# A decoder trunk in fp32r: every tile that products read moves to a multiple of 512 bytes in its partition

## The chip, the cores and the metric

The kernel runs on one core of a Trainium2 chip. The metric is the device time of one execution in microseconds (us). Before the change three runs gave 3106.07, 3107.32 and 3114.94 us, a median of 3107.32. One more execution was taken with the profiler; its own time is 3115.24 us, and its span from the first to the last instruction 3113.5 us.

A core has five engines that run side by side and wait for each other through semaphores: TensorE (PE in the profile, with the weight loads apart as PEld), VectorE (DVE), ScalarE (ACT), GpSimd (POOL) and SyncE (SP), which here only issues DMAs. SBUF is the on-chip memory of 128 partitions; a tile [P, N] takes N elements in each of the 128 partitions, at the same byte offset in all of them. PSUM is the memory that TensorE writes.

## What is computed

Two decoder layers over 1024 tokens of width 1024, all in fp32. Each layer computes `x <- LN(alpha*x + mixer(x))` and then `x <- LN(alpha*x + MLP(x))`, the MLP with 4096 hidden units and a squared ReLU. The mixer of layer 0 is a gated DeltaNet with 8 heads of 128 (short convolution on q, k and v, then a chunked delta rule); that of layer 1 is S5, a complex diagonal state-space layer. Beside each mixer runs a 4-head cross-attention into 256 memory tokens, and both share an input and an output projection. For the change, S5 matters: 64 groups of 16 channels each drive 64 complex states,

```
h_t = Abar * h_(t-1) + Bbar u_t        (per group, elementwise in the state)
y_t = Re(C h_t) + D u_t
```

## The kernel before, in words

**Products.** A weight or activation that goes into a wide product is split into a high part, rounded to the type fp32r, and a low part, the rest, also fp32r. `mm3` (lines 111 to 116) then makes one fp32 product of three fp32r products, high x high, high x low and low x high, added up in PSUM. The wide products have 128 x 128 weights and 512 moving columns; those of the memory keys (mk) and of the attention scores (sc) have 256. `proj_fm` (line 122) multiplies 128 output features at a time with the transposed activations xT: 8 slices of 128 input features, two halves of 512 tokens, so 48 products for one block of weights. `acc_tm` (line 138) multiplies token tiles with the second MLP weights or the output projection and adds to y. DeltaNet's chunk products and S5's are in plain fp32 and have 128 columns; the trace shows two PE instructions for each of those.

**Order.** `run` (line 1165) goes through: the first input projections and gates; memory keys and values and attention of layer 0 among the first DeltaNet keys; the eight DeltaNet heads (`gdn_b`, with `conv_silu` at line 384 for q, k and v); the output projection and layer norm; the first MLP (14 blocks of two hidden tiles and one of four); memory keys and values of layer 1; S5 with the attention of layer 1; the GLU; the second output projection; the second MLP. PE works through its products in that order. Beside the first MLP, `s5_side` (line 1254) puts the preparation of S5 behind each MLP block: tables, coefficients (`s5_coeffs`) and the matrices of S5 (`s5_mats`, line 1039), which POOL's DMA queue writes to DRAM.

**S5.** A sequence of 1024 tokens is cut into 128 chunks of 8, so that time runs over 128 columns, and a tile has 8 groups. `s5_u` (line 1067) projects the input of 8 groups and writes it to DRAM as ud; `s5_core` (line 1077) of the same 8 groups loads it as u. In u each group has a row of 129 columns: column 0 is set to zero by DVE (line 1083), columns 1 to 128 are the 128 chunks (line 1084). The products p1 and p2 (lines 1107 to 1110) read columns 0 to 127, the chunk before; DVE's scan (line 1118) runs the state over the columns; three products add up to py: M0, which works within a chunk, reads columns 1 to 128 of u (line 1125), and H1 and H2 read the rotated states r1 and r2 (lines 1126, 1127). H1 comes from `combine` (line 1002) in `s5_mats`: three DVE operations over [128, 4 groups, 9 lags, 16], 576 elements, in the tag h5. Lags 0 to 7 go into the product pz (line 1052), followed for each group by a product with dd, which DVE makes after H1 (line 1136); lags 1 to 8 are what `s5_core` later loads (line 1099). POOL's queue writes all nine to DRAM in one DMA (line 1048).

**Memory.** Two pools lie in SBUF, constants (`cp`) and then work tiles (`sp`). The work pool has a fixed number of buffers per tag (line 50), each as long as the tag's longest tile; every tile of a tag lies in one of its buffers. The allocator goes in steps of 32 bytes. The program of the kernel before has these byte offsets, given as the rest after division by 512:

| tag or tile | what lies there | length of a buffer | offset within 512 |
|---|---|---|---|
| ident (constant) | identity for transposes, at 16512 | 512 | 128 |
| scr | masks, gate values, S5 powers, at 17984 | 5280 | 64 |
| h1, raw, w1 | second MLP weights (half), loads, first weights | 2048, 4096, 4096 | 224 |
| xT (6 buffers) | activations high and low, keys, y, S5's s5t | 16448 | 224, 288, 352, 416, 480, 32 |
| gb (2) | convolution input, norms, S5 coefficients | 4128 | 96, 128 |
| S (6) | DeltaNet's states and the like, dd | 512 | 160 |
| h5 (5) | S5 matrices, some MLP weights | 2304 | 160, 416 in turn |
| h2, h3, h4 | second MLP weights (half), hidden parts, attention | 2048 | 416 |

Slices that products take within a tile begin at multiples of 512 bytes from the tile's start, with these exceptions: u's rows in s5t (129 columns, 516 bytes apart, read from column 0 or column 1), H1's groups (576 bytes apart), and weights of 32 columns or fewer.

Of the kernel before, what the change touches and what calls it, by code (L numbers as in the profile page):

```python
# [10 lines left out]
F32 = mybir.dt.float32  # L11
# [5 lines left out]
P = 128  # L17
T = 1024
# [10 lines left out]
class Trunk:  # L29
    def __init__(self, ctx, tc, a):  # L30
        self.tc = tc
        self.nc = nc = tc.nc
        self.a = a
        self.uid = 0
        self.turn = 0
        self.proj = 0
        self.cp = ctx.enter_context(tc.tile_pool(name="cp", bufs=1))
        self.sp = ctx.enter_context(tc.tile_pool(name="sp", bufs=1))
        self.ps = ctx.enter_context(tc.tile_pool(name="ps", bufs=1, space=bass.MemoryType.PSUM))
        self.dp = ctx.enter_context(tc.tile_pool(name="dp", bufs=1, space=bass.MemoryType.DRAM))  # L40
        self.ident = self.const("ident", [P, P])
        make_identity(nc, self.ident)
        self.eps_ln = self.const("eps_ln", [P, 1])
        nc.gpsimd.memset(self.eps_ln, 1e-5)
        self.mhalf = self.const("mhalf", [P, 4])
        nc.gpsimd.memset(self.mhalf, -0.5)
        self.half = self.const("half", [P, 4])
        nc.gpsimd.memset(self.half, 0.5)
# [172 lines left out]

    def gdn_consts(self):
        nc = self.nc
        scr = self.tile("scr", [P, 3 * P + 8 + 13 * 64 + 96], F32, "scr")
        masks = [scr[:, n * P:(n + 1) * P] for n in range(3)]
        self.small = [scr[:, 3 * P + 8 + n * 64:3 * P + 8 + (n + 1) * 64] for n in range(13)]
        early = self.tile("h1", [P, 3 * P], F32, "early")
        U = early[:, 0:P]
        nc.gpsimd.memset(U, 1.0)
        nc.gpsimd.affine_select(U, U, [[1, P]], ALU.is_ge, 0.0, base=0, channel_multiplier=-1)  # L230
        self.U = U
        ones = early[:, P:2 * P]
        nc.gpsimd.memset(ones, 1.0)
        self.ones = ones
        mn = masks[0]
        nc.gpsimd.memset(mn, 0.0)
        nc.gpsimd.affine_select(mn, mn, [[1, P]], ALU.is_ge, -1e30, base=0, channel_multiplier=-1)
        self.maskneg = mn

        m64 = masks[1]  # L240
        nc.gpsimd.memset(m64, 0.0)
        nc.gpsimd.memset(m64[0:32, 32:64], 1.0)
        nc.gpsimd.memset(m64[64:96, 96:128], 1.0)
        m128 = masks[2]
        nc.gpsimd.memset(m128, 0.0)
        nc.gpsimd.memset(m128[0:64, 64:128], 1.0)
        self.m64, self.m128 = m64, m128
        bd = scr[:, 3 * P:3 * P + 4]
        nc.gpsimd.memset(bd, 0.0)
        for b in range(4):  # L250
            nc.gpsimd.memset(bd[32 * b:32 * b + 32, b:b + 1], 1.0)
        self.bdm = bd
        self.early = [early[:, 2 * P + 64 * n:2 * P + 64 * (n + 1)].rearrange("p (t h) -> p t h", t=8) for n in range(2)]
        cw = scr[:, 3 * P + 8 + 13 * 64:].rearrange("p (m j) -> p m j", j=4)
        nc.sync.dma_start(cw, self.a["cw"])
        self.cw = cw
        ng = self.const("ng", [P, 1])
        nc.sync.dma_start(ng, self.a["ng"])
        nc.gpsimd.tensor_scalar(ng, ng, 0.5, None, op0=ALU.mult)
        self.ng = ng  # L260
        self.kdd = self.dp.tile([8, 2, P, 4, P], F32, tag="kdd", name="kdd")
        self.ded = self.dp.tile([8, 2, P, 4, P], F32, tag="ded", name="ded")
        self.ntf = self.dp.tile([8, 2, 2, P, 4, P], F32, tag="ntf", name="ntf")
        self.ntd = self.dp.tile([8, 8, 4, 32, 32], F32, tag="ntd", name="ntd")
        self.t32 = self.dp.tile([2, 8, 8, 4, 32, 32], F32, tag="t32", name="t32")
# [118 lines left out]
    def conv_silu(self, m, xT, outs, tag, w=None):  # L384

        nc = self.nc
        cv = self.tile("gb", [P, 3 + T], F32, "cv")
        nc.vector.memset(cv[:, 0:3], 0.0)

        def evac(h, ps):  # L390
            b = h * HALF
            nc.scalar.copy(cv[:, 3 + b:3 + b + HALF], ps)
            o = outs[h]
            w = self.cw[:, m, :]
            nc.scalar.activation(o, ps, AF.Copy, scale=w[:, 3:4])
            for j in range(3):
                nc.vector.scalar_tensor_tensor(o, cv[:, b + j:b + j + HALF], w[:, j:j + 1], o, op0=ALU.mult, op1=ALU.add)
            th = self.tile(tag, [P, HALF], F32, "th")
            nc.scalar.activation(th, o, AF.Tanh, scale=0.5)
            nc.vector.scalar_tensor_tensor(o, th, 1.0, o, op0=ALU.add, op1=ALU.mult)  # L400

        self.proj_fm(w or self.a["w_in"][m], xT, evac, "wi")
# [596 lines left out]
        nc.gpsimd.memset(z, 0.0)  # L999
        nc.gpsimd.dma_start(self.zd[:, :, :, 0:112].rearrange("m i g x -> (m i) g x"), z)  # L1000

    def combine(self, eng, x, y, pr, pi, op, b, nm):

        n = pr.shape[1]
        o, w = (self.tile("h5", [P, 4, n, 16], F32, z) for z in (nm, "cw"))
        gs = slice(4 * b, 4 * b + 4)
        xb, yb = (z[:, gs, :].unsqueeze(2).to_broadcast([P, 4, n, 16]) for z in (x, y))
        pr, pi = (z.rearrange("p d g -> p g d").unsqueeze(3).to_broadcast([P, 4, n, 16]) for z in (pr, pi))
        eng.tensor_tensor(o, xb, pr, op=ALU.mult)
        eng.tensor_tensor(w, yb, pi, op=ALU.mult)  # L1010
        eng.tensor_tensor(o, o, w, op=op)
        return o
# [26 lines left out]
    def s5_mats(self, m, b, co):  # L1039

        nc = self.nc
        V = nc.vector
        A_, S_ = ALU.add, ALU.subtract
        flat = lambda x: x.rearrange("p a b -> p (a b)")
        re, im = (z[:, :, 8 * m:8 * m + 8] for z in self.pw)
        gs = gl = slice(4 * b, 4 * b + 4)
        h1 = self.combine(V, co[:, 2], co[:, 3], re[:, :, gl], im[:, :, gl], A_, b, "H1")
        nc.gpsimd.dma_start(self.h1d[m, :, gs], h1)
        dd = self.dd(8 * m + 4 * b)
        pz = self.psum("pa", "pz", (P, 4, 8, 16))  # L1050
        for g in range(4):
            nc.tensor.matmul(flat(pz[:16, g]), co[:, 0, 4 * b + g, :], flat(h1[:, g, 0:8, :]), start=True, stop=False)
            nc.tensor.matmul(pz[:16, g, 0, :], self.ident[:16, :16], dd[:, g, :], start=False, stop=True)
        z = self.tile("h5", [P, 4, 8, 16], F32, "z")[:16]
        nc.scalar.copy(z, pz[:16])
# [21 lines left out]
    def s5_core(self, m):  # L1077

        nc = self.nc
        V, G = nc.vector, nc.gpsimd  # L1080
        M, A_ = ALU.mult, ALU.add
        u = self.s5t[:, 2 * T + 8 * 129 * (m % 2):2 * T + 8 * 129 * (m % 2 + 1)].rearrange("p (g n) -> p g n", g=8)
        V.memset(u[:, :, 0:1], 0.0)
        nc.sync.dma_start(u[:, :, 1:129], self.ud[m].rearrange("s (i g) n -> (s i) g n", i=16))
        M0 = self.s5t[:, T:2 * T].rearrange("p (g x) -> p g x", g=8)
        z = self.zd[m]
        nc.sync.dma_start(M0, bass.AP(z.tensor, z.offset, [[16, 8], [8 * 240, 16], [240, 8], [1, P]]))
        for b in range(2):
            gs = slice(4 * b, 4 * b + 4)
# [7 lines left out]
            G1 = load("h1", "G1", self.g1d[m, :, gs])  # L1097
            tab = [load("h2", "tab", self.tabd[x, :, g0:g0 + 4, :]) for x in range(2)]
            H1 = load("h2", "H1", self.h1d[m, :, gs, 1:9, :].rearrange("p g d o -> p g (d o)"))
            H2 = load("h2", "H2", self.h2d[m, :, gs])  # L1100

            p1 = self.psum("pa", "p1", (P, 4, P))
            p2 = self.psum("pa", "p2", (P, 4, P))
            G2 = self.tile("h1", [P, 4, P], F32, "G2")
            nc.scalar.copy(G2[:, :, 0:64], G1[:, :, 64:128])
            nc.scalar.copy(G2[:, :, 64:128], G1[:, :, 0:64])
            for g in range(4):
                nc.tensor.matmul(p1[:, g, :], G1[:, g], u[:, 4 * b + g, 0:128], start=True, stop=True)
            for g in range(4):
                nc.tensor.matmul(p2[:, g, :], G2[:, g], u[:, 4 * b + g, 0:128], start=True, stop=True)  # L1110
            t1 = self.tile("h3", [P, 4, P], F32, "t1")
            t2 = self.tile("h3", [P, 4, P], F32, "t2")
            V.tensor_tensor(t1, p1, tab[0], op=M)
# [2 lines left out]
            w = self.tile("h3", [P, 4, P], F32, "wsc")  # L1116
            for g in range(4):
                V.tensor_tensor_scan(w[:, g, :], self.r8[:, g0 + g:g0 + g + 1].to_broadcast([P, P]), t1[:, g, :], 0.0, M, A_)
            r1 = self.tile("h1", [P, 4, P], F32, "r1")
            r2 = self.tile("h1", [P, 4, P], F32, "r2")  # L1120
# [1 line left out]
            G.tensor_tensor(r2, w, tab[1], op=M)  # L1122
            py = self.psum("pi", "py", (P, 4, P))
            for g in range(4):
                nc.tensor.matmul(py[:, g, :], M0[:, 4 * b + g, :], u[:, 4 * b + g, 1:129], start=True, stop=False)
                nc.tensor.matmul(py[:, g, :], H1[:, g], r1[:, g, :], start=False, stop=False)
                nc.tensor.matmul(py[:, g, :], H2[:, g], r2[:, g, :], start=False, stop=True)  # L1127
            zg = self.tile("h3", [P, 4, P], F32, "zg")
            nc.scalar.activation(zg, py, AF.Gelu_apprx_tanh)
            nc.sync.dma_start(self.yd[m].rearrange("s (o g) n -> (s o) g n", o=16)[:, gs, :], zg)  # L1130
# [34 lines left out]
    def run(self):  # L1165
# [39 lines left out]
        self.cat = d("cat1", [1536, T])  # L1205
        xT = self.mlp_block(0, y, xT, self.s5_side, lambda tau: nc.sync.dma_start(self.x2[tau], y[tau]), True)
        kv = self.mem_kv(1)
        self.s5t = self.tile("xT", [P, 2 * T + 2 * 8 * 129], F32, "s5t")
        self.s5_u(0, xT)
        for m in range(8):  # L1210
            if m < 7:
# [129 lines left out]
```

## Time and profile before

| | before |
|---|---|
| median of three runs | 3107.32 us |
| the profiled execution, its own time | 3115.24 us |
| its span | 3113.5 us |
| instructions | 36492 |
| mean granted TensorE clock | 0.967 of full |
| DMA | 288.11 MB in 204145 packets |

How to read the views that follow. The page's first lines give each engine's busy time and its share of the span, then, as a digit for each of 40 slices, tenths of full speed for the clock. The view of stretches has one row per stretch of time: its length, then busy microseconds and, in brackets, the instruction count of PE, PEld, DVE, ACT and POOL, the granted clock, the DMA share and GB/s. The view of groups has one row per line, engine and operands: shape, count, then busy time, mean ns of one instruction, idle time of its engine just before, and who ended it. The view of order gives start, duration, engine, line and operands, with `x8` where neighbours of one kind are merged. Matmuls are pipelined: one is under way while the next starts, so a duration is not the time that one more costs; the difference of two starts is.

### The profile page before, as it was taken

To read this page: it belongs to the slowest core of one execution; us is meant where nothing else is said; L and a number is where in the kernel's file an instruction comes from. 1 tells how busy PE (TensorE), PEld (TensorE's weight loads), DVE (VectorE), ACT (ScalarE), POOL (GpSimd) and SP (SyncE) were. 2 spreads that over 40 slices of the span, in tenths; PEclk is the share of its full clock that TensorE was granted. 3 is DMA by queue.
4 is the path that set the end of the run, shared out by engine and by line. 5 is a ranking of instruction groups with operands and counts; after the bars stand their busy time and mean duration, and the time that the engine had idled before them with its cause. 6 is when DMAs were issued, how large, how long until landed. Compare 5 with 4: busy or idle time off the path is not lost. (4 is left out here: it accounts for less than half of the span.)

```text
span 3113.5 us, 36492 instructions
## 1 busy us (share of the span) xinstructions
PE 2892.1 (93%) x13629; PEld 2311.9 (74%) x13629; DVE 1762.9 (57%) x3452; ACT 964.6 (31%) x2070; POOL 488.4 (16%) x729
## 2 busy tenths in 40 slices
PE   8789898898998999999999989987999999999998
PEld 6568676676777888777777767765777888888876
DVE  7635766765578677666663733443467344334436
ACT  5334444443422322232222222332222222222221
POOL 3620633625001021110100100011000000000001
PEclk9889999999999999999999999998999999999999
DMA  5322433333522133222221365554321111111111
GB/s 193 101 58 82 115 105 101 99 105 77 179 82 76 42 108 92 83 97 73 87 85 62 103 183 168 167 144 142 108 95 61 48 48 43 53 48 48 41 48 54
DMA packets 204145, 288.11 MB, mean 93 GB/s; under 512 B 85776, under 2 KB 126944, under 8 KB 203968
## 3 DMA queue, kind: packets, MB, share of 16 engines
q1 hardware_dynamic: 188864, 245.46, 25.7%
q0 software_dynamic: 12800, 36.13, 3.9%
q10 hardware_dynamic: 2304, 4.20, 0.4%
q8 instruction: 107, 1.75, 0.2%
q14 instruction: 70, 0.57, 0.1%
HBM read 213.93 MB, written 71.79 MB: 92 GB/s over the span
## 5 line engine op out<-in xcount | busy, mean ns | idle before, releaser
L213 DVE TENSOR_TENSOR y<-tm,y 128x512 f32<-128x512 f32 x448 | 308.5, 690 | 223.0 <-PE tm L116 217.4
L114 PE MATMUL w<-xTh,w1h 128*128 128x512 f32 x1024 | 409.7, 400 | 14.9 <-ACT w1h L93 14.9
L116 PE MATMUL w<-xTh,w1l 128*128 128x512 f32 x1024 | 407.4, 398 | 4.5 <-DVE w1l L94 4.4
L114 PE MATMUL tm<-w2h,hh 128*128 128x512 f32 x1024 | 406.7, 398 | 0.0
L115 PE MATMUL w<-xTl,w1h 128*128 128x512 f32 x1024 | 406.6, 397 | 0.0
L116 PE MATMUL tm<-w2h,hl 128*128 128x512 f32 x1024 | 403.6, 395 | 0.0
L115 PE MATMUL tm<-w2l,hh 128*128 128x512 f32 x1024 | 402.1, 393 | 0.0
L106 ACT CAST w2h<-w2r 128x512 fp32r<-128x512 f32 x128 | 76.3, 619 | 588.7 <-PE tm L116 506.0
L114 PEld LDWEIGHTS w<-xTh,w1h 128*128 128x128 f32 x1024 | 194.1, 190 | 60.0 <-ACT w1h L93 16.2
L116 PEld LDWEIGHTS w<-xTh,w1l 128*128 128x128 f32 x1024 | 194.5, 190 | 52.0 <-DVE w1l L94 6.3
L115 PEld LDWEIGHTS w<-xTl,w1h 128*128 128x128 f32 x1024 | 194.2, 190 | 45.1
L116 PEld LDWEIGHTS tm<-w2h,hl 128*128 128x128 f32 x1024 | 192.1, 188 | 47.4 <-DVE hl L202 0.3
L114 PEld LDWEIGHTS tm<-w2h,hh 128*128 128x128 f32 x1024 | 192.2, 188 | 45.8 <-ACT hh L201 1.3
L115 PEld LDWEIGHTS tm<-w2l,hh 128*128 128x128 f32 x1024 | 192.7, 188 | 44.7
L167 POOL TENSOR_SCALAR mv<-mv 128x1 f32<-128x1 f32 x32 | 25.0, 780 | 1246.8 <-DVE mv L166 1246.8
L202 DVE TENSOR_TENSOR hl<-w,hh 128x512 fp32r<-128x512 f32 x128 | 87.2, 687 | 188.6 <-ACT hh L201 188.6
L94 DVE TENSOR_TENSOR w1l<-w1r,w1h 128x1024 fp32r<-128x1024 f32 x64 | 78.3, 1224 | 184.7 <-ACT w1h L93 184.7
L114 PE MATMUL wi<-xTh,wih 128*128 128x512 f32 x384 | 159.3, 415 | 3.5 <-ACT zc L640 3.5
L115 PE MATMUL wi<-xTl,wih 128*128 128x512 f32 x384 | 158.7, 413 | 0.0
L116 PE MATMUL wi<-xTh,wil 128*128 128x512 f32 x384 | 156.4, 407 | 0.0
L197 ACT ACTIVATE w<-w 128x512 f32<-128x512 f32 x128 | 74.5, 582 | 188.0 <-PE w L116 188.0
L93 ACT CAST w1h<-w1r 128x1024 fp32r<-128x1024 f32 x64 | 67.2, 1050 | 198.8 <-PE w L115 157.4
(414 smaller groups left out, 5791.3 us busy)
## 6 DMA issues: line engine op xcount, KB each, us to landing
w2r<-in_w_dram SPq DMA_DIRECT2D x64, 512.0 KB, 3.5
w1r<-in_w_dram SPq DMA_DIRECT2D x64, 512.0 KB, 3.5
wir<-in_w_in_dram SPq DMA_DIRECT2D x24, 512.0 KB, 3.7
wor<-in_w_o_dram SPq DMA_DIRECT2D x24, 512.0 KB, 3.5
cat<-cat SPq DMA_DIRECT2D x24, 512.0 KB, 3.4
gb<-gcd SPq DMA_DIRECT2D x32, 256.0 KB, 4.5
ntf<-nm POOLq DMA_DIRECT2D x32, 256.0 KB, 3.0
nm<-ntf SPq DMA_DIRECT2D x32, 256.0 KB, 3.4
```

The costliest lines, as they stand in the source:

```text
L93: nc.scalar.copy(hi, r)
L94: nc.vector.tensor_tensor(lo, r, f32(hi), op=ALU.subtract)
L106: nc.scalar.copy(hi, s)
L114: nc.tensor.matmul(ps, a[0], b[0], start=start, stop=False)
L115: nc.tensor.matmul(ps, a[0], b[1], start=False, stop=False)
L116: nc.tensor.matmul(ps, a[1], b[0], start=False, stop=stop)
L167: nc.gpsimd.tensor_scalar(mv[:, 2:3], mv[:, 1:2], 1e-5, None, op0=ALU.add)
L197: nc.scalar.activation(ps, ps, AF.Relu)
L202: nc.vector.tensor_tensor(lo, ps, f32(hi), op=ALU.subtract)
L213: nc.vector.tensor_tensor(o, ps, o, op=ALU.add)
```

## The change

The constants are padded, and the work pool begins at 18432: a tile of 448 bytes is added behind ident, and the constants then add up to 1920 bytes from 16512. Buffers whose length was no multiple of 512 become one: scr 5632 bytes, gb 4608, xT 16384, h5 2048. The lengths of the others stay. For xT, S5's u has rows of 128 columns without the zero column: p1 and p2 read all 128, so their states are those of one chunk later, and the shift by one chunk moves to H1 and H2, which multiply columns 0 to 126 of r1 and r2 and write columns 1 to 127 of py. For h5, H1 is made in two calls of `combine`: lags 0 to 7 in h5 as before, lag 8 in the tag S (three DVE operations over 64 elements), each with a DMA of its own on POOL's queue. The memset of u's zero column goes, and the load of u fills a contiguous piece of 4 KB in each partition.

```diff
         make_identity(nc, self.ident)
+        self.const("pad", [P, 112])
         self.eps_ln = self.const("eps_ln", [P, 1])
...
-        scr = self.tile("scr", [P, 3 * P + 8 + 13 * 64 + 96], F32, "scr")
+        scr = self.tile("scr", [P, 11 * P], F32, "scr")[:, :3 * P + 8 + 13 * 64 + 96]
...
-        cv = self.tile("gb", [P, 3 + T], F32, "cv")
+        cv = self.tile("gb", [P, T + P], F32, "cv")[:, :3 + T]
...
-    def combine(self, eng, x, y, pr, pi, op, b, nm):
+    def combine(self, eng, x, y, pr, pi, op, b, nm, tag="h5"):
         n = pr.shape[1]
-        o, w = (self.tile("h5", [P, 4, n, 16], F32, z) for z in (nm, "cw"))
+        o, w = (self.tile(tag, [P, 4, n, 16], F32, z) for z in (nm, "cw"))
...
-        h1 = self.combine(V, co[:, 2], co[:, 3], re[:, :, gl], im[:, :, gl], A_, b, "H1")
-        nc.gpsimd.dma_start(self.h1d[m, :, gs], h1)
+        h1 = self.combine(V, co[:, 2], co[:, 3], re[:, 0:8, gl], im[:, 0:8, gl], A_, b, "H1")
+        nc.gpsimd.dma_start(self.h1d[m, :, gs, 0:8], h1)
+        h8 = self.combine(V, co[:, 2], co[:, 3], re[:, 8:9, gl], im[:, 8:9, gl], A_, b, "H8", "S")
+        nc.gpsimd.dma_start(self.h1d[m, :, gs, 8:9], h8)
...
-            nc.tensor.matmul(flat(pz[:16, g]), co[:, 0, 4 * b + g, :], flat(h1[:, g, 0:8, :]), start=True, stop=False)
+            nc.tensor.matmul(flat(pz[:16, g]), co[:, 0, 4 * b + g, :], flat(h1[:, g]), start=True, stop=False)
...
-        u = self.s5t[:, 2 * T + 8 * 129 * (m % 2):2 * T + 8 * 129 * (m % 2 + 1)].rearrange("p (g n) -> p g n", g=8)
-        V.memset(u[:, :, 0:1], 0.0)
-        nc.sync.dma_start(u[:, :, 1:129], self.ud[m].rearrange("s (i g) n -> (s i) g n", i=16))
+        u = self.s5t[:, (2 + m % 2) * T:(3 + m % 2) * T].rearrange("p (g n) -> p g n", g=8)
+        nc.sync.dma_start(u, self.ud[m].rearrange("s (i g) n -> (s i) g n", i=16))
...
-                nc.tensor.matmul(p1[:, g, :], G1[:, g], u[:, 4 * b + g, 0:128], start=True, stop=True)
+                nc.tensor.matmul(p1[:, g, :], G1[:, g], u[:, 4 * b + g, :], start=True, stop=True)
...
-                nc.tensor.matmul(p2[:, g, :], G2[:, g], u[:, 4 * b + g, 0:128], start=True, stop=True)
+                nc.tensor.matmul(p2[:, g, :], G2[:, g], u[:, 4 * b + g, :], start=True, stop=True)
...
-                nc.tensor.matmul(py[:, g, :], M0[:, 4 * b + g, :], u[:, 4 * b + g, 1:129], start=True, stop=False)
-                nc.tensor.matmul(py[:, g, :], H1[:, g], r1[:, g, :], start=False, stop=False)
-                nc.tensor.matmul(py[:, g, :], H2[:, g], r2[:, g, :], start=False, stop=True)
+                nc.tensor.matmul(py[:, g, :], M0[:, 4 * b + g, :], u[:, 4 * b + g, :], start=True, stop=False)
+                nc.tensor.matmul(py[:, g, 1:], H1[:, g], r1[:, g, 0:P - 1], start=False, stop=False)
+                nc.tensor.matmul(py[:, g, 1:], H2[:, g], r2[:, g, 0:P - 1], start=False, stop=True)
...
-        self.s5t = self.tile("xT", [P, 2 * T + 2 * 8 * 129], F32, "s5t")
+        self.s5t = self.tile("xT", [P, 4 * T], F32, "s5t")
```

## The prediction

> **What bounds the kernel now.** I read the page first, then the busy time by stretch, then the costliest groups, then the order of time inside a few streams of products.
>
> ```profile
> PE 2892.1 (93%) x13629; PEld 2311.9 (74%) x13629; DVE 1762.9 (57%) x3452; ACT 964.6 (31%) x2070; POOL 488.4 (16%) x729
> PEclk9889999999999999999999999998999999999999
> ```
>
> ```profile
> core 0: us, PE busy (x) PEld busy (x) DVE busy (x) ACT busy (x) POOL busy (x), PEclk, DMA share, GB/s
> 205.00:818.00 613.00, 546.75 (x2939) 435.29 (x2937) 386.10 (x849) 272.50 (x787) 215.98 (x299) 0.97 0.35 102
> 818.00:988.00 170.00, 165.03 (x802) 132.35 (x802) 128.01 (x233) 49.10 (x124) 7.03 (x14) 0.98 0.30 92
> 988.00:1780.00 792.00, 770.38 (x3477) 607.34 (x3475) 521.30 (x1158) 215.12 (x356) 105.65 (x199) 0.99 0.25 82
> 1815.00:2125.00 310.00, 257.55 (x1425) 213.27 (x1423) 130.27 (x267) 92.09 (x195) 33.62 (x22) 0.94 0.59 169
> 2369.00:3105.00 736.00, 723.05 (x3088) 583.43 (x3088) 320.16 (x446) 180.40 (x289) 16.58 (x18) 0.99 0.15 51
> ```
>
> The stretches are the DeltaNet heads, the first output projection, the first MLP, S5 and the second MLP. In both MLPs PE is busy 97 to 98% of the time (770.38 of 792, 723.05 of 736) at a granted clock of 0.99, and DVE at most 66%. So TensorE's stream of products sets the end, and what counts is how often a product can start.
>
> ```profile
> L114 PE MATMUL w<-xTh,w1h 128*128 128x512 f32 x1024 | 409.7, 400 | 14.9 <-ACT w1h L93 14.9
> L114 PE MATMUL tm<-w2h,hh 128*128 128x512 f32 x1024 | 406.7, 398 | 0.0
> L114 PE MATMUL wi<-xTh,wih 128*128 128x512 f32 x384 | 159.3, 415 | 3.5 <-ACT zc L640 3.5
> L114 PE MATMUL tm<-woh,ch 128*128 128x512 f32 x240 | 96.9, 405 | 7.2 <-ACT ch L831 7.2
> L114 PE MATMUL tm<-woh,chl 128*128 128x512 f32 x144 | 59.0, 411 | 3.3 <-ACT chl L831 3.3
> L114 PE MATMUL wz<-xTh,wzh 128*128 128x512 f32 x128 | 53.9, 421 | 4.3 <-ACT vT L395 4.1
> L114 PE MATMUL wq<-xTh,wqh 128*128 128x512 f32 x128 | 53.7, 420 | 0.0
> L114 PE MATMUL wg<-xTh,wgh 128*128 128x512 f32 x128 | 51.7, 404 | 14.2 <-ACT wgh L93 14.2
> L114 PE MATMUL wu<-xTh,wuh 128*128 128x512 f32 x128 | 51.0, 399 | 0.0
> ```
>
> Each is one of three products that mm3 (lines 114 to 116) issues equally often, so the nine rows stand for 3 x (1024 + 1024 + 384 + 240 + 144 + 4 x 128) = 9984 products of 512 columns: 6144 in the MLPs, 1152 + 384 in the output projections and the GLU, 2304 in the DeltaNet and S5 stretches. Their 400 ns are latency: successive products overlap. The price of one more is the step from start to start, which the order of time shows (first and last row of an unbroken stream):
>
> ```profile
> 1555.74 0.39 PE L115 MATMUL tm<-w2l,hh 128*128 128x512 f32 x1
> ...
> 1557.84 0.40 PE L115 MATMUL tm<-w2l,hh 128*128 128x512 f32 x1
> ```
>
> ```profile
> 1833.72 0.39 PE L114 MATMUL wu<-xTh,wuh 128*128 128x512 f32 x1
> ...
> 1836.96 0.40 PE L116 MATMUL wu<-xTh,wul 128*128 128x512 f32 x1
> ```
>
> ```profile
> 48.29 0.28 PE L115 MATMUL mk<-meml,wkh 128*128 128x256 f32 x1
> ...
> 49.43 0.28 PE L116 MATMUL mk<-memh,wkl 128*128 128x256 f32 x1
> ```
>
> ```profile
> 139.82 0.28 PE L115 MATMUL sc<-kv,qh 128*128 128x256 f32 x1
> ...
> 141.25 0.28 PE L115 MATMUL sc<-kv,qh 128*128 128x256 f32 x1
> ```
>
> ```profile
> 1731.02 1.09 PE L180 MATMUL xt<-ident,y 128*128 128x128 f32 x8
> 1731.87 0.48 PE L115 MATMUL tm<-w2l,hh 128*128 128x512 f32 x1
> ```
>
> ```profile
> 1837.20 1.05 PE L1108 MATMUL p<-s5t,G 128*128 128x128 f32 x8
> 1838.09 0.61 PE L1110 MATMUL p<-s5t,G 128*128 128x128 f32 x4
> ```
>
> ```profile
> 1860.53 1.05 PE L1108 MATMUL p<-s5t,G 128*128 128x128 f32 x8
> 1861.42 0.61 PE L1110 MATMUL p<-s5t,G 128*128 128x128 f32 x4
> ```
>
> The MLP stream takes 9 steps in 2.10 us, 233 ns each; wu 14 in 3.24, 231 ns. With 256 columns, mk takes 10 steps in 1.14, 114 ns, and sc 12 in 1.43, 119 ns. Two things are to be seen. A 512-column product costs 5 ns more than two mk products although it loads weights once and not twice. And mk and sc, equal in shape and type, differ by 5 ns with nothing between them but their addresses. So the step holds something beside columns, and addresses move it.
>
> **Where the operands lie.** The table in the section on the kernel gives the offsets. All wide operands of before lie at 32 beyond a multiple of 64, none at a multiple of 64, 128, 256 or 512. Among themselves they take seven different offsets within 512, and steps stay at 231 to 233 ns; so the trace says that one odd offset is as good as another, and says nothing of an even one. After the change, by the sizes in the diff, the shared pool begins at 16512 + 1920 = 18432 = 36 x 512, every tag's buffers are multiples of 512 long, and all 9984 products read both operands at multiples of 512. Only ident (offset 128) and narrow weights as in line 1052 don't.
>
> **The change, part by part.**
>
> 1. The step of the 9984 products. Its end on the dear side is no change, 0 ns. A middle row is mk: at its rate per column a 512-column step is 228, 5 ns less. The far end is from the transposes, whose moving operand, ident, lies at 128, a multiple of 64 (that a transpose is no product may matter as well): 8 in 0.85 us, 106 ns for 128 columns, against 111 ns for a pass of line 1108 (8 in 0.89). An MLP step is 2.1 such passes; if it were two transposes' worth, 2 x 106 = 212, 21 ns less. I take the middle of 228 and 212 (nearest to neither, and both are rows of the same engine): 220, or 12 to 13 ns less; 12. MLPs: 6144 x 12 = 73.7, times 0.975 for PE's share = 72. Output projections and GLU: 1536 x 12 = 18.4, times 0.96 = 18. DeltaNet and S5: 2304 x 12 = 27.6; there PE also waits, so times 0.85 (546.75 of 613, 257.55 of 310) = 23. Sum 113 us. What is late next: DVE, with 521 us in an MLP stretch that would shrink to about 752; still no bound.
>
> [...]
>
> 2. H1 cut into eight lags and one (lines 1047, 1048). The rows:
>
> ```profile
> L1010 DVE TENSOR_TENSOR cw<-co,pw 128x512 f32<-128x512 f32 x32 | 21.9, 685 | 13.1 <-PE pg L1060 11.4 <-DMA h2d<-H 1.5
> L1010 DVE TENSOR_TENSOR cw<-co,pw 128x576 f32<-128x576 f32 x16 | 12.1, 753 | 0.8 <-issue 0.5
> L1136 DVE TENSOR_TENSOR dd<-ident,dsk 16x64 f32<-16x64 f32 x16 | 2.7, 206 | 0.0
> ```
>
> ```profile
> L1048 POOL DMA_DIRECT2D h1d<-H x16: 539/542/547, 1273.2 to 1631.9; - x16
> ```
>
> Three operations of 753 become three of 685 (-0.20 us) and three of 64 elements, for which dd is the nearest row (+0.62): +0.42 us on DVE, 16 times, 6.7 us, beside an MLP in which DVE has 271 us to spare. H1 is ready 0.2 us earlier; dd, behind the three new ones on DVE, 0.42 us later, and PE's second product at line 1053 waits for it, with the whole MLP queued in order behind. At worst 6.7 us of PE; I take 2, since line 1052's two passes run meanwhile. The extra DMA is 16 x 0.54 = 9 us of POOL, which works 106 of those 792 us, and more, smaller pieces; line 1094 reads the result some 190 us later at the least (1631.9 against 1815). Cost nothing; without that cover a few us for each load.
>
> 3. S5's input. Eight DVE memsets go, the load becomes one run of 4 KB per partition where it was eight of 512 bytes, and it stands ahead of M0's load on SP's queue.
>
> ```profile
>   DMA s5t<-zd: 9.8, 4
> ```
>
> PE, ACT and DVE together waited 9.8 us for M0 (view of the tile s5t). Gain between 0 and 10; I take 2. The shift itself moves into lines 1126 and 1127 (127 columns of 128 and an output one word on): a hundredth of 256 short passes, nothing.
>
> 4. DVE, ACT and DMA on the new addresses: nothing, since they lie beside PE; between -5 and +5.
>
> Sum: -113 + 2 - 2 = -113. The profiled execution took 3115.24 (span 3113.5), which gives 3002; the median of the runs is 3107.3, 8 lower, and gives 2994. I forecast **2995 us**, with its own range 2930 to 3060: 3107 less 180 (212 ns everywhere) and less 47 (228).
>
> **The rivals.**
>
> *Nothing to be had.* The step is the products' own, and an even offset is as good as an odd one. For it: seven odd offsets agree, and line 1108 holds a small test. In the stream from 1837.20 the four rows of u start at 480, 484, 488 and 492 within 512, in that from 1860.53 at 0, 4, 8 and 12; both take 0.89 us. Against it: those are passes of 111 ns per 128 columns, half as fast per column as the wide ones, so a slow read may hide in them. Time: 3107 with 2 and 2 of parts 2 and 3, within 10 of it. [...]
>
> *Same offset, same bank.* Weights are loaded while the product before streams; where both begin at the same offset they may ask for the same piece of memory at once. For it: sc, whose operands are both at 416, steps by 119 ns, mk, at 416 and 224, by 114. The change puts all operands at one offset. Price 5 ns for each of 9984, 50 us: 3157. Against it: the MLP stream above alternates between w2 tiles at 224 and at 416 with weights at 416, and holds 233. It decides if the step of tm and w rises over 233.
>
> *A part of it*: only what mk shows goes, 5 ns: 47 us, 3060; it lies in my forecast's range.
>
> **How the numbers follow.** A measurement of this kernel tells about 0.3% (9 us) from no change. Forecast with its lower part: 0.6. Nothing to be had: 0.18. Same offset, same bank, or a cost in PE's order larger than mine: 0.22. Range 2930 to 3140: below lies 0.05 (more than 212 ns would give), above some 0.14 of the slower case.
>
> **What would show it.** Right: steps of tm and w at 212 to 228 ns with counts unchanged, both MLP stretches 15 to 60 us shorter each, and PE's share little changed. Wrong: steps of 231 to 233 (nothing), or above (same bank); steps that fall while stretches don't, with DVE or a DMA as the releaser before w or tm. For part 2: a wait of PE at line 1053 on DVE dd over 2 us. For part 3: the row of waits on s5t<-zd.

## The result, and the profile after

Four runs of the changed kernel gave 3067.55 to 3077.65 us, median 3070.74; the kernel before gave 3108.95 beside them. The ratio is 0.9878, with an interval of 0.9854 to 0.9901: 38 us faster. The forecast was 2995, 113 faster. The sign was right, the size three times too large.

The page of the changed kernel, first its busy times, then its clock by slice:

```profile
PE 2847.4 (93%) x13629; PEld 2306.5 (75%) x13629; DVE 1764.3 (58%) x3492; ACT 966.1 (32%) x2070; POOL 503.9 (16%) x745
...
PEclk9889999999999999999999999997999999999999
```

The stretches of the changed kernel, cut at the same events as those of before:

```profile
core 0: us, PE busy (x) PEld busy (x) DVE busy (x) ACT busy (x) POOL busy (x), PEclk, DMA share, GB/s
205.00:809.00 604.00, 540.90 (x2941) 430.74 (x2939) 384.31 (x850) 273.78 (x788) 216.60 (x299) 0.98 0.35 103
809.00:973.00 164.00, 160.46 (x802) 130.45 (x803) 127.38 (x233) 49.00 (x123) 7.10 (x14) 1.00 0.31 95
973.00:1765.00 792.00, 760.72 (x3474) 608.54 (x3474) 522.55 (x1205) 214.31 (x355) 121.93 (x214) 0.98 0.25 81
1798.00:2104.00 306.00, 257.47 (x1428) 214.86 (x1427) 130.69 (x263) 92.81 (x196) 33.57 (x22) 0.94 0.56 172
2342.00:3059.00 717.00, 704.42 (x3088) 581.91 (x3088) 319.31 (x446) 180.37 (x289) 15.79 (x17) 0.99 0.16 52
```

The second MLP shrinks from 736 to 717 us, the output projection from 170 to 164, the DeltaNet heads from 613 to 604, S5 from 310 to 306. **The first MLP does not move: 792 and 792.** Its products are the same as those of the second MLP; PE is busy 10 us less in it and idle 10 us more.

The order of time of the changed kernel, first and last rows of unbroken streams (a first-layer product `w`, a second-layer product `tm`, then the 256-column `mk` and `sc`):

```profile
2500.30 0.39 PE L117 MATMUL w<-xTh,w1l 128*128 128x512 f32 x1
...
2503.02 0.39 PE L117 MATMUL w<-xTh,w1l 128*128 128x512 f32 x1
2503.25 0.39 PE L115 MATMUL tm<-w2h,hh 128*128 128x512 f32 x1
...
2505.97 0.39 PE L115 MATMUL tm<-w2h,hh 128*128 128x512 f32 x1
```

```profile
48.01 0.28 PE L115 MATMUL mk<-memh,wkh 128*128 128x256 f32 x1
...
49.21 0.28 PE L116 MATMUL mk<-meml,wkh 128*128 128x256 f32 x1
```

```profile
140.26 0.28 PE L116 MATMUL sc<-kv,qh 128*128 128x256 f32 x1
...
141.70 0.28 PE L116 MATMUL sc<-kv,qh 128*128 128x256 f32 x1
```

w takes 12 steps in 2.72 us, tm the same: 226.7 ns, where before had 233. mk takes 10 steps in 1.20, 120 ns, where before had 114: **it became slower.** sc stays (12 in 1.44, 120). Averaged over all unbroken neighbours in the order of time (starts 205 to 255 ns apart, before and after): w 232.5 to 227.1, tm of the MLPs 232.5 to 226.9, tm of the output projections 232.3 to 227.6, wg 231.8 to 226.7, wu 231.4 to 227.5, wq 230.9 to 228.7, wi 230.6 to 229.0, wz 230.5 to 229.1. By the counts of the prediction: MLPs 3072 x 5.4 + 3072 x 5.6 = 34 us, output projections and GLU 1152 x 4.7 + 384 x 5.1 = 7, the rest 4 to 5. That is some 45 us of gain at TensorE. The result has 38, and other things, below, are mixed into it.

PE's waits in the first MLP, before, then after:

```profile
PE pg L1060 <- ACT z L1055: 1.2, 2, 0.6
PE pz L1052 <- DVE H L1011: 1.1, 1, 1.1
```

```profile
PE pz L1055 <- DVE H L1012: 7.2, 8, 1.6
PE w L115 <- ACT w1h L94: 5.9, 1, 5.9
PE w L117 <- DVE w1l L95: 4.8, 1, 4.8
PE pg L1063 <- DVE G1T L1012: 2.2, 1, 2.2
PE pg L1063 <- ACT z L1058: 0.7, 1, 0.7
```

The columns are total us, times, longest. The waits of w were there before (5.8 and 4.4). Those of pz and pg, S5's matrices, grew from 2.3 to 10.1 us. Added up from the order of time, from the last wide product ahead of pz or pg to the first behind, these places take 46.1 us in 29 goes before, 59.7 us in 37 goes after: **+13.6 us in the first MLP**. Each of the eight more goes takes in one step of a wide product that was there before too (1.8 us together), so the loss is some 12 us.

A further loss follows two of these pauses:

```profile
1469.96 1.09 PE L1063 MATMUL pg<-ident,G1T 128*128 128x128 f32 x4 [2.24 <-DVE G1T L1012]
...
1471.28 0.63 PE L116 MATMUL w<-xTl,w1h 128*128 128x512 f32 x1
1471.70 0.63 PE L117 MATMUL w<-xTh,w1l 128*128 128x512 f32 x1
```

The granted clock is 0.5 for 3.4 us from 1315.7 and from 1469.2 us, and the step is 0.42 us there in place of 0.23. The kernel before has no such dip in this part of its first MLP. Of all kernels run here, the nine with the cut ahead of dd show one at one or both of these places, the others none. Before has 53 steps longer than 255 ns between neighbouring wide products of that MLP, the changed kernel 70; at 0.2 us each for the 17 more that is an estimate of 3 us. With the 12 us this is nearly all of what the steps gave in the first MLP (some 17 us).

DVE and POOL in the same place after (the second view: duration in ns, smallest, median, largest):

```profile
DVE cw L1011 <- DMA zd<-z: 10.5, 7, 2.6
```

```profile
L1049 POOL DMA_DIRECT2D h1d<-H x16: 767/772/785, 1252.2 to 1618.8; - x16
L1051 POOL DMA_DIRECT2D h1d<-H x16: 750/756/765, 1254.8 to 1610.3; - x16
```

DVE now waits 10.5 us for the store of z, and each h1d store takes 0.77 and 0.76 us of POOL where the single one took 0.54. In S5, the view of the tile s5t after:

```profile
  DMA s5t<-zd: 6.1, 2
```

It was 9.8 in 4 waits.

### The profile page after: what moved, and what is told of

Read it like the earlier page. It is cut to its first block, busy times and chain, and to the rows that moved or that the text cites. A ratio compares the mean times of both kernels' runs of the same rounds, so it can differ in the third digit from the quotient of the medians.

```text
span 3065.5 us, 36560 instructions
## 1 busy us (share of the span) xinstructions
PE 2847.4 (93%) x13629; PEld 2306.5 (75%) x13629; DVE 1764.3 (58%) x3492; ACT 966.1 (32%) x2070; POOL 503.9 (16%) x745
## 3 DMA queue, kind: packets, MB, share of 16 engines
q1 hardware_dynamic: 181696, 245.46, 25.6%
q10 hardware_dynamic: 2304, 4.20, 0.4%
## 5 line engine op out<-in xcount | busy, mean ns | idle before, releaser
L115 PE MATMUL tm<-w2h,hh 128*128 128x512 f32 x1024 | 399.0, 390 | 0.1
L117 PE MATMUL tm<-w2h,hl 128*128 128x512 f32 x1024 | 397.3, 389 | 0.0
```

The source lines that it names most:

```text
L115: nc.tensor.matmul(ps, a[0], b[0], start=start, stop=False)
L117: nc.tensor.matmul(ps, a[1], b[0], start=False, stop=stop)
```

## The experiments

**What the operands have to be: e1, e2.** The theory behind the prediction says that a tile's own start matters, even against odd. The rival that grew out of mk's 114 to 120: only the relation of the two operands matters. e1 moves every tile by 32 bytes, so that all of them are as odd as before, yet equal.

```diff
-        self.const("pad", [P, 112])
+        self.const("pad", [P, 120])
```

> After, with the pad 32 bytes longer: every work tile at 32 within 512, all still at one offset. If the rest within 64 (or 512) is what counts: the step of the wide products goes back from 226.7 to about 232 ns, 9984 x 5.5 = 55 us, 3125 us. If only the relation of the two operands counts (all at one offset): step 226.7, 3070 us.

e2 puts scr, h1, raw and w1 at 256 within 512 and leaves the rest at 0:

```diff
-        self.const("pad", [P, 112])
+        self.const("pad", [P, 48])
...
+        self.tile("pd", [P, 64], F32, "pd")
```

> After, with scr, h1, raw and w1 at 256 within 512 and all else at 0: the weights of w, wi, wu, wg and the moving w2 tiles in h1 lie half a unit away from the other operand. If the rest within 64 is what counts: all steps stay at 226.7, 3070 us. If the relation counts: the step of w changes (back to 231 to 233, or lower still), and that of tm for half of its products; at 6 ns for three in four of 9984 products, 45 us: 3115 us, or 3025 if the sign is the other.

Streams of w, e1 and then e2:

```profile
2500.19 0.39 PE L115 MATMUL w<-xTh,w1h 128*128 128x512 f32 x1
...
2505.86 0.39 PE L116 MATMUL w<-xTl,w1h 128*128 128x512 f32 x1
```

```profile
2500.24 0.39 PE L116 MATMUL w<-xTl,w1h 128*128 128x512 f32 x1
...
2505.90 0.39 PE L117 MATMUL w<-xTh,w1l 128*128 128x512 f32 x1
```

25 steps take 5.67 and 5.66 us: 227 ns in both. e1 3082.48 us, ratio 0.9903 (0.9883 to 0.9923); e2 3070.03, 0.9863 (0.9844 to 0.9881). The prediction's theory falls: tiles at 32 within 512 step as fast as tiles at 0. The relation counts, and a distance of 256 bytes is as good as none. That e1 is slower than e2 by 12 us at an equal step was not explained by either theory; e12 to e14 take it up.

**Which distances cost: e5, e6, e7, e10.** The same edit with other sizes puts scr, h1, raw and w1 at 448, 384, 320 and 480 within 512, the rest at 0: distances of 64, 128, 192 and 32 bytes between w's operands. Each ran in one execution.

```diff
-        self.const("pad", [P, 112])
+        self.const("pad", [P, 96])
...
+        self.tile("pd", [P, 16], F32, "pd")
```

> After, with scr, h1, raw and w1 at 448 within 512 and all else at 0: the two operands of w and the half of tm's products with w2 in h1 lie 64 bytes apart within 256. If what cost 6 ns before was that the operands' offsets differ by 64, 128 or 192: the step of w goes back to 231 to 233 ns and tm's between, about 3115 us. If it was something else (the odd lengths of the buffers, the boundaries that a tile crosses): 226.7, 3070 us.

> The same with 384 within 512, so 128 bytes apart. If any difference within 256 costs: steps of 231 to 233 in w; if only 64 and 192 do: 226.7. About 3115 or 3070 us.

> The same with 320 within 512, so 192 apart, the relation of tm and mk in the kernel before. If the relation decides: tm and w at 231 to 233 ns and mk at 114 instead of 120, as before. If not: 226.7 and 120.

> After with scr, h1, raw and w1 moved 32 bytes back against the rest (480 and 0 within 512). If any unequal remainder of 256 bytes costs, wide products with weights from raw and w1 take 229 to 233 ns and those of 256 columns 113 to 119, time some 3100 to 3120. If the remainder is told only by units of 64 bytes, the step lies at 226.7 or at the value of a distance of 192 (231 to 233.3), time 3071 in the first case. If small distances cost in proportion, something between 226.7 and 229.

Streams of w at a distance of 64 (e5) and of 32 (e10):

```profile
2506.65 0.40 PE L115 MATMUL w<-xTh,w1h 128*128 128x512 f32 x1
...
2512.25 0.40 PE L115 MATMUL w<-xTh,w1h 128*128 128x512 f32 x1
```

```profile
2511.19 0.39 PE L115 MATMUL w<-xTh,w1h 128*128 128x512 f32 x1
...
2516.79 0.39 PE L115 MATMUL w<-xTh,w1h 128*128 128x512 f32 x1
```

24 steps in 5.60 us, 233 ns, in both. Over the whole run w averages 232.0, 232.4, 233.3 and 233.2 ns at 64, 128, 192 and 32 bytes. The times are 3106.37, 3109.3, 3119.09 and 3109.55 us, where before had medians of 3114.9 and 3114.8 on those chips: by these single executions nearly all of the gain is gone, with every tile still at a multiple of 32, 64 or 128. mk goes the other way, 116, 119, 115 and 117 ns against 120 in the changed kernel; the 119 at 128 bytes can hardly be told from it. One limit: in streams that mix distances (tm alternates between weights of both kinds) also the products whose own operands agree take 229 to 233 ns, so what was seen is a property of a stream, not of one product.

**What the cut of H1 costs: e4, e3, e11.** e4 is the kernel before with the cut alone (one work tile in h5 is declared longer, so that the tag keeps its 2304 bytes).

```diff
...
-        h1 = self.combine(V, co[:, 2], co[:, 3], re[:, :, gl], im[:, :, gl], A_, b, "H1")
-        nc.gpsimd.dma_start(self.h1d[m, :, gs], h1)
+        h1 = self.combine(V, co[:, 2], co[:, 3], re[:, 0:8, gl], im[:, 0:8, gl], A_, b, "H1")
+        nc.gpsimd.dma_start(self.h1d[m, :, gs, 0:8], h1)
+        h8 = self.combine(V, co[:, 2], co[:, 3], re[:, 8:9, gl], im[:, 8:9, gl], A_, b, "H8", "S")
+        nc.gpsimd.dma_start(self.h1d[m, :, gs, 8:9], h8)
...
```

> Before, with H1 cut in two as in the change and nothing else; addresses as before. If the split holds PE up: 13 to 17 us more than before, 3124 us, all of it in the first MLP. If not: 3109 us.

PE's waits in the first MLP of e4:

```profile
PE pz L1054 <- DVE H L1011: 5.5, 8, 1.5
...
PE pg L1062 <- DVE G1T L1011: 2.9, 2, 2.3
```

3123.86 us, ratio 1.0034 (1.0022 to 1.0045), that is 11 us slower; the first MLP takes 805 us against 791 before, pz and pg 57.3 us in 37 goes, and the clock dips twice for 6.8 us at the places where the changed kernel dips. So the cut costs 11 to 14 us by itself, at the old steps.

e3 is the changed kernel with H8's three operations and its DMA moved behind H2, the last work of `s5_mats`:

```diff
-        h8 = self.combine(V, co[:, 2], co[:, 3], re[:, 8:9, gl], im[:, 8:9, gl], A_, b, "H8", "S")
-        nc.gpsimd.dma_start(self.h1d[m, :, gs, 8:9], h8)
         dd = self.dd(8 * m + 4 * b)
...
         nc.gpsimd.dma_start(self.h2d[m, :, gs], h2.rearrange("p g e o -> p g (e o)"))
+        h8 = self.combine(V, co[:, 2], co[:, 3], re[:, 8:9, gl], im[:, 8:9, gl], A_, b, "H8", "S")
+        nc.gpsimd.dma_start(self.h1d[m, :, gs, 8:9], h8)
```

> After, with lag 8 of H1 (three DVE operations and its DMA) moved from before dd to the end of s5_mats. If the split holds PE up in the first MLP: the time of PE in and around pz falls from 59.7 us to about the 46 us of before, the two clock dips there go, 3056 us. If the first MLP's missing gain has another cause: 3070 us.

3059.86 us, ratio 0.9836 (0.9812 to 0.986). The first MLP takes 778 us, pz and pg 47.1 us in 29 goes, and the two dips are gone. e11 moves the DMA alone and leaves the three operations where they are:

```diff
-        nc.gpsimd.dma_start(self.h1d[m, :, gs, 8:9], h8)
         dd = self.dd(8 * m + 4 * b)
...
+        nc.gpsimd.dma_start(self.h1d[m, :, gs, 8:9], h8)
```

> After with the DMA of H8 alone moved to the end of its block's matrices; the three VectorE operations of H8 stay where they are, ahead of G1's and G2's combinations. Theory Q (the wait grows on POOL's queue: two issues in place of one stand ahead of the stores that free combine's buffers): PE's time in and around pz falls from 59.7 to about 47 us, the wait of pz on H from 7 to about 1, time about 3060 as in e3. Theory V (the three operations on VectorE stand ahead of what pz and pg wait for): 57 to 60 us remain, time about 3070.

Waits of PE, then of DVE, in the first MLP of e11:

```profile
PE pz L1054 <- DVE H L1012: 6.7, 8, 1.8
PE pg L1062 <- DVE G1T L1012: 2.0, 1, 2.0
```

```profile
DVE cw L1011 <- DMA zd<-z: 10.1, 7, 3.0
```

3072.78 us, ratio 0.9873 (0.9853 to 0.9893), the first MLP at 794, with both dips: nothing regained. Theory Q, the longer issues on POOL's queue, falls; the three operations on DVE, where they stand, are the cause. The order of time shows how they work. PE in the changed kernel, then at the same place in e3:

```profile
1608.67 0.38 PE L1055 MATMUL pz<-H,co 128*16 128x128 f32 x2
1608.98 0.50 PE L115 MATMUL w<-xTh,w1h 128*128 128x512 f32 x1
1609.42 0.21 PE L1056 MATMUL pz<-dd,ident 16*16 16x16 f32 x2
```

```profile
1602.88 0.39 PE L116 MATMUL w<-xTl,w1h 128*128 128x512 f32 x1
1603.36 0.38 PE L1053 MATMUL pz<-H,co 128*16 128x128 f32 x2
1603.67 0.21 PE L1054 MATMUL pz<-dd,ident 16*16 16x16 f32 x2
```

In the changed kernel a wide product stands between pz's first passes and the product with dd, in 8 of the 16 blocks: the program's own order on PE has changed, not only its timing. From 1608.67 to 1609.42 are 0.75 us, in e3 0.31 (1603.36 to 1603.67), and the wide product in between is worth 0.23 of it. The 0.21 left over, 8 times, is an estimate of 1.7 us. The larger part is the wait that e11 has and e3 hardly has: H2's `cw` on DVE waits for the store of z (10.5 us in 7 waits in the changed kernel, 1.1 in 2 in e3), since `cw` takes a buffer of h5 that z had; so the next block's H1 is late, and PE waits for it (the row of pz on H; the waits at pz and pg grew by 7.8 us). The two were not tried apart, nor were the dips.

**S5's new load alone: e8.** The kernel before with u's rows of 128 columns and the shift on the states, nothing else.

```diff
...
-        V.memset(u[:, :, 0:1], 0.0)
-        nc.sync.dma_start(u[:, :, 1:129], self.ud[m].rearrange("s (i g) n -> (s i) g n", i=16))
...
+        nc.sync.dma_start(u, self.ud[m].rearrange("s (i g) n -> (s i) g n", i=16))
...
```

> Before, with only S5's u changed (rows of 128, no memset, the shift at the states; s5t at its old length, so all other addresses as before). If the shorter load of u ends M0's wait: the S5 stretch loses 4 to 7 us, 3105 us. If S5's gain came from the steps alone: 3111 us.

3112.49 us, ratio 0.9995 (0.9983 to 1.0006). The hardware queue moves 181696 packets in place of 188864 for the same bytes, and the wait for s5t<-zd stays at 10.2 us in 4 waits: nothing gained that can be measured.

**Relation without the cut: e9.** If 256 bytes are enough, H1 can stay whole (2304 = 9 x 256) and the constant pad can go.

```diff
-        scr = self.tile("scr", [P, 3 * P + 8 + 13 * 64 + 96], F32, "scr")
+        scr = self.tile("scr", [P, 21 * 64], F32, "scr")[:, :3 * P + 8 + 13 * 64 + 96]
...
-        cv = self.tile("gb", [P, 3 + T], F32, "cv")
+        cv = self.tile("gb", [P, T + 64], F32, "cv")[:, :3 + T]
...
-        self.s5t = self.tile("xT", [P, 2 * T + 2 * 8 * 129], F32, "s5t")
+        self.s5t = self.tile("xT", [P, 4 * T], F32, "s5t")
```

> Before with the scratch at 21 x 64 numbers, the convolution's pad at T + 64, S5's new u tile, no constant pad, and H1 left in one piece: 9 x 256 bytes, so that every tile of products starts at 64 or at 320 within 512 bytes, one remainder of 256. Theory (what decides is whether weights and moving operand have the same remainder of 256 bytes, whatever it is; and the cut of H1 costs some 11 to 14 us): the wide step is 226.7 ns, products of 256 columns 120, the time of PE in and around pz is 46 to 47 us in 29 stretches, and the time is 3055 to 3062, below after's 3071 and about e3's 3060. Rival (a distance of 256 bytes between tiles also costs, and e2 was luck of its four tags): steps of 228 to 233, time 3075 to 3110.

Steps of 227.0 (w) and 119.8 (mk), pz's wait on H down to 0.3 us, the first MLP at 780: all as expected. The time was not: 3068.61 us, ratio 0.9855 (0.9838 to 0.9871). Its S5 stretch takes 313 us where the changed kernel has 305 (starts of the same products), and the wait for s5t<-zd is 10.9 us. Its tiles start at 64 and 320 within 512; e1's start at 32.

**The start of a tile, apart from the relation: e12, e13, e14.** The kernel of e3 with all tiles at 256, at 64 and, again, at 0, on one chip.

```diff
-        self.const("pad", [P, 112])
+        self.const("pad", [P, 48])
```

> e3 (H8's work last) with the constant pad cut from 112 to 48 numbers: every tile of products starts at 256 within 512 bytes in place of 0; the relation of the operands is the same. Theory T (the start of a tile within 512 bytes sets how long transfers take that land in it, and S5 and the streaming of weights pay): if 256 is as good as 0, time 3056 to 3063 beside e14's, the wait of py on s5t<-zd 6 to 7 us, ud<-s5t landing in 3.1 to 3.3 us; if transfers want a multiple of 512, 3066 to 3073, wait 10, landing 3.7. Rival N (e9 and e1 lie higher by chance or for other reasons of theirs): no difference from e14 whatever the start. In each case wide steps of 226.7 ns.

> e3 with no constant pad: every tile of products starts at 64 within 512 bytes. Theory T: 3066 to 3073, that is 7 to 12 us over e14, wait of py on s5t<-zd about 10 us in 3 or 4 times, ud<-s5t landing in 3.7 to 4.1 us. Rival N: within 3 us of e14. Wide steps 226.7 ns by both.

> The kernel of e3 again (every tile of products at a multiple of 512 bytes, H8's work last), as the one that e12 and e13 are held against on the same chip: 3056 to 3063, ratio to before 0.982 to 0.985.

The tile s5t, waits and landing times of its transfers, in e14 (at 0) and in e13 (at 64):

```profile
  DMA s5t<-zd: 6.1, 2
...
DMA to landing us min/median/max: 3.0/3.3/5.2
```

```profile
  DMA s5t<-zd: 9.0, 3
...
DMA to landing us min/median/max: 3.4/3.9/5.1
```

e14 3057.73 us, ratio 0.9823 (0.981 to 0.9837); e12 3058.82, 0.9831 (0.9818 to 0.9844); e13 3068.63, 0.9855 (0.9837 to 0.9873). w steps by 227.0 ns in all three. So 256 is as good as 0, and 64 costs about 10 us. The intervals of e13 and e14 only just touch, that of e12 overlaps e13's a little, and one of e13's four runs came at 3058.57; but e1 and e9 point the same way, and with tiles at 32, 64 or unaligned the waits for s5t<-zd are 9 to 11 us, at 0 or 256 they are 6 to 8.

In the profiled runs 6 of e13's 14 us stand in S5 and 3 in the memory keys and values before it; e3, the same kernel as e14, differs from it by 3 and 4 us in these two stretches. The stores ud<-s5t land after 3.1 us in e14, 3.2 in e12 and 3.5 in e13, where 3.7 to 4.1 was expected for e13. Over all runs the transfers of s5t land after 3.2 to 3.4 us (median) with s5t at 0 or 256, and after 3.9 to 4.6 otherwise, with one exception: e5, whose s5t is at 0, has 3.9 and a wait of 8.1 us. So later landing goes with tiles off a multiple of 256 in most profiles; that this is where the 10 us come from is not shown.

The kernel of e3 and e14 beats both kernels of the case: 55 us under before.

## Why the prediction was right or wrong

**Step 1, the 9984 steps: right that addresses move them, wrong in size and in cause.** The sum took 12 ns for each; it is 4 to 6 ns in the MLPs, the output projections, the GLU and wu, and about 2 in wi, wz and wq. The measured 226.7 lies almost on the middle row, mk's 228, but that is luck: mk's 114 came with unequal operands, and the change that brought the wide step to 226.7 took mk itself to 120. What failed is the far end: the 212 ns was taken from transposes, which take 109 ns on average before and after the change and told nothing of a product's addresses, and the forecast went halfway towards it. (The low end of the range was also mis-summed: 21 ns for each, with the same discounts, is 198 us and not 180.) MLPs 34 us in place of 72, projections and GLU 7 in place of 18, DeltaNet and S5 4 in place of 23. Why wi and wz gain so little was not tested; in the changed kernel about half of wi's steps (398 of 745) take 226 or 227 ns as elsewhere, and most of the others 228 to 241. The cause was wrong too: the text read "one odd offset is as good as another, and says nothing of an even one". Odd or even is nothing (e1: 227 ns with every tile at 32); whether the operands of a stream agree in their remainder of 256 bytes is what counted for 512 columns (w at 227 ns in e2, at 232.0 to 233.3 in e5 to e7 and e10). The table of offsets held that: in every 512-column stream of before the operands lay apart or alternated. That the time fell was luck in part, since a move to multiples of 512 also makes all operands equal. No 512-column stream of the changed kernel averages under wg's 226.7 ns, so the 212 was reached nowhere.

**Step 2, the cut of H1: mis-sized, 2 us for 11 to 14.** The durations were right: three operations of 206 ns were priced, and the trace has 206 to 213 ns each on average. The bound of 6.7 us was no bound, because it counted only the operations' own time ahead of dd. Left out were that the order on PE would change with them, that z's store, delayed, holds a buffer that DVE needs before the next block (waits of 10.1 us in e11, 1.1 in e3), and the clock dips behind the pauses (0.5 for 3.4 us, twice). POOL's DMAs were priced at 0.54 and took 0.77 and 0.76, hidden as said (e11).

**Step 3, S5's input: -2, near enough.** Alone nothing (e8). The wait for M0 does fall, from 9.8 to 6.1 us, but not through the load; with the start of the tile alone it differs by 3 us (e13, e14, one profile each).

**Step 4, DVE, ACT and DMA on the new addresses: priced at nothing, and by the difference of e13 and e14 worth about 10 us in the kernel's favour.**

Together: -45 from the steps, +1 from mk (192 products by 6 ns), +13 from the cut, -10 from the tiles' start if the kernel before pays for it what e13 pays (an estimate; before was not run so): about -41 against the measured -38.

**The rivals.** *Nothing to be had* is refuted: the step of w fell from 232.5 to 227.1, and a distance of 256 bytes between its operands in place of 32 changes it from 233 (e10) to 227 (e2). *Same offset, same bank* had the right variable and, for 512 columns, the wrong sign: with equal operands w takes 227.1 ns, with unequal ones 232.0 to 233.3 (e5 to e7, e10). For the 256 columns from which it was read it holds: mk went from 114 to 120, and back to 116 and 115 in e5 and e7. The reading of sc was wrong, though: in the stream that the prediction shows, of layer 0, the program has the moving kv at 32 and the weights at 416, 128 bytes apart; only in layer 1 are both at 416. The two take 118.9 and 119.5 ns on average, and the changed kernel, where all are equal, 119.3: sc tells nothing for or against. *A part of it*, mk's 5 ns, 3060, came nearest, by the coincidence named in step 1.

**Of what would show it:** the steps of tm and w fell into 212 to 228 and the second MLP lost 19 us; the first MLP lost none. The sign named for part 2, a wait of PE for dd over 2 us, did not come: the wait that grew was of pz on H.

## What to carry to other kernels

For streams of wide fp32r products, compare the starts of weights and moving operand modulo 256 bytes before asking whether each is aligned by itself; here equal starts were worth 4 to 6 ns of 232 for each in most streams, and cost no copy. When an edit puts work ahead of something on a loaded engine, its own duration does not bound its cost (here 6.7 us of DVE time, as priced, cost 11 to 14): look for the buffer that is released later and for the instruction that now slips in between. A row serves as a bound only when it is known why it differs: mk was cheaper because its operands were unequal (114 ns, and 120 with equal ones), the transposes are another operation (109 ns before and after), and neither told what equal operands do to a product of 512 columns.

## What the runs showed of the hardware

- With equal remainders of 256 bytes between weights and moving operand the 512-column step of w, wg and the MLPs' tm averages 226.7 to 227.1 ns in every kernel that was run; with unequal or mixed ones these average 229 to 233 (distances of 32, 64, 128 and 192 bytes). At 256 columns mk goes the other way: 120 with equal remainders, 114 to 117 at distances of 32, 64 and 192, 119 at 128 (mk in e6, sc of layer 0 in the kernel before). fp32 passes (111 to 112 ns a pass for u) and transposes (109) stayed as they were.
- Transfers of S5's tile landed after 3.2 to 3.4 us (median) with the tile at 0 or 256 within 512 (3.9 in one run, e5), and after 3.9 to 4.6 with tiles at 64, at 32 or as before.
- Behind two pauses of PE in the changed kernel's first MLP the granted clock fell to 0.5 for 3.4 us, and the step of w rose from 0.23 to 0.42 us.
- A DMA that writes eight of nine lags of h1d takes 772 ns of POOL, one that writes a single lag 756, one that writes all nine 542.
